# A sixth product in seven quarters, added onto banks that hold a result, with GpSimd adding kept halves

## The chip, the cores and the metric

The kernel runs on one core of a Trainium2 chip. A core has TensorE (PE, matmuls; PEld is its weight loads), VectorE (DVE), ScalarE (ACT), GpSimd (POOL) and SyncE (SP, whose queue issues the DMAs), an on-chip memory (SBUF, 128 partitions) and eight PSUM banks of 128 x 512 fp32, into which matmuls write. The metric is device time in microseconds, the median of several runs; lower is better.

## The reference

```python
def reference(x, w):          # x: 8 x 2048 x 2048, w: 2048 x 2048, float32
    cs = np.cumsum(x, axis=1)
    diff = cs - np.concatenate([zeros, cs[:, :-1, :]], axis=1)
    return np.matmul(diff, w).astype(np.float32)
```

The difference of a running sum is x itself, so what is computed is x times w: 16384 rows by 2048 by 2048.

## The kernel before

The rows are 128 tiles of 128. Four are done plainly, four by `group_plain`, and the remaining 120 by 30 calls of `group(g)`, four tiles each: g, g+1, h = g+2 and h+1. These calls are the periods 1 to 30 of the order list.

**Outer scheme.** The rows are scaled to fp16 and turned (DMA transposes), the right side w is kept in fp16 with one scale. A group multiplies pairs of tiles by the 2 x 2 blocks of w with Strassen's scheme in Winograd's form: seven products with the right sides B11, B21, T1, T2, T3, B22, T4 instead of eight. The left sides are A11, A12, S1, S2, S3, S4, A22, each for g and for h. S1 = A21 + A22, S2 = S1 - A11, S3 = A11 - A21, S4 = A12 - S2, made by DVE (`total`, 128 x 1024 fp16). X and Y are the bank pairs of A11 B11 for g and h; onto these S2 T2 and then S3 T3 are added by matmuls that start with `start=False`. At each stage the value is kept (ACT, `keep`) or added to kept results (DVE, `add`, a scaled add from a bank to SBUF).

**Inner scheme.** Five of the seven products are themselves done in seven quarter products (class `Quarters`, P1 = A11 B11, P2 = A12 B21, P5 = S1 T1, P3 = S4 B22, P4 = A22 T4): the rows g and h make the two rows of blocks, the halves of the depth and of the columns the rest. One product takes seven slots of four matmuls of 128 x 128 by 128 x 512. Its left sums s1 to s4 are made by DVE in small `rooms`; its right-hand differences Q1 to Q4 stand in SBUF (`spare`), or are made anew for each use by `give` into the one buffer `flow`. ACT copies the partial sum in the first bank out (`first`, `out2`, `out4`), DVE adds such copies back into banks (`middle`, `last`).

```python
(h[0], "a11", "t11", True),      # the seven slots of Quarters: bank, left, right, start
(h[1], "s1", "Q1", True),
(h[0], "s2", "Q2", False),
(g[0], "a12", "t21", False),
(h[0], "s3", "Q3", False),
(g[1], "s4", "t22", False),
(h[0], "a22", "Q4", False),
```

The two remaining products, S2 T2 and S3 T3, are whole: the list `steps` of `group` holds their pieces of four matmuls, 16 matmuls for each of S2g T2, S2h T2, S3g T3, S3h T3, and `go` issues the next ones. In period 1 P1 is whole too (`plainly`).

**Rows in.** `load`, `weigh` (ACT, the row's absolute sum, 128 x 1024), `scale_of` (a mean on ACT, a reciprocal on DVE, the unit on ACT), `narrow` (ACT, to fp16) and `turn` (DMA) bring the next group's tiles in. `put` stores results.

**Order.** `record` notes each operation with a label, an engine and a function that issues it; `emit` sorts all of them by a key from the dictionary `places` (by period and label, `None` for the periods without a list of their own), and `after` fixes that order on each engine. So each engine's order is written out by hand, and an engine runs it in order, each instruction behind its own waits.

## Time and profile before

| | |
|---|---|
| runs | 1447.86, 1449.06, 1449.23 us; median 1449.06 us |
| profiled execution | span 1446.9 us from the first to the last instruction; the runs' times lie 1.0 to 2.3 us above it |
| PE, DVE, ACT, POOL busy | 1439.8, 1339.8, 1193.8, 0.9 us |
| granted clock | 0.999 mean |
| DMA | 351.59 MB, mean 243 GB/s |

A row of a table by stretches gives the stretch and its length, the busy time of each engine with its number of instructions, the granted clock, the share of DMA and its rate. A row of a group gives line, engine, operation, what is written and read with shapes, the count, the busy time in us and the mean of one in ns, then the idle time before such instructions and what ended it. A row of the timeline gives start, length and the instruction. Most helpers record through one line, so that L590 is every two-operand DVE operation, L649 the scaled add, L145 and L141 ACT's scaled and plain copies, L602 and L624 the matmuls of whole and of quarter products.

### The profile page before, as it was taken

The numbers are of one execution on the slowest core, as the hardware profiler recorded it, in microseconds if no ns is written. First come the engines' busy times: TensorE is split into PE (matmuls) and PEld (weight loads), VectorE is DVE, ScalarE is ACT, GpSimd is POOL, SyncE is SP. The second block draws the span as 40 slices with busy tenths as digits, with TensorE's granted clock in tenths as the row PEclk, the third lists the DMA queues.
The fourth block names the chain that finished last, engine by engine and source line by source line (L and its number), as shares of the span: only waits on it lengthen the run. The fifth ranks groups of instructions, "written<-read, shape, count | busy, mean of one in ns | idle before, by whom it ended". The sixth has DMA issues, their size and how long they took to land.

```text
span 1446.9 us, 20369 instructions
## 1 busy us (share of the span) xinstructions
PE 1439.8 (100%) x6698; PEld 652.8 (45%) x6698; DVE 1339.8 (93%) x2355; ACT 1193.8 (83%) x1985; POOL 0.9 (0%) x5
## 2 busy tenths in 40 slices
PE   9999999999999999999999999999999999999998
PEld 4444444444444444444444444444444444444443
DVE  7999999999999999999999999999999999999988
ACT  4897878898888888888988888988888888889783
POOL 0000000000000000000000000000000000000000
PEclk9999999999999999999999999999999999999999
DMA  9999988899888999988898989998989998899963
GB/s 362 375 266 265 250 227 222 230 249 264 231 229 223 243 256 241 242 227 229 245 263 219 245 220 242 245 264 217 236 231 242 265 236 237 216 235 249 275 190 116
DMA packets 343930, 351.59 MB, mean 243 GB/s; under 512 B 270992, under 2 KB 270992, under 8 KB 343824
## 3 DMA queue, kind: packets, MB, share of 16 engines
q1 hardware_dynamic: 343824, 350.29, 89.4%
q8 instruction: 52, 0.85, 0.2%
q14 instruction: 54, 0.44, 0.1%
HBM read 150.99 MB, written 134.22 MB: 197 GB/s over the span
## 4 chain that ended last, share of the span: by engine, by line
PE 93%; issue 4%; DVE 1%; ACT 1%; DMA 0%; POOLq 0%; DVEq 0%
PE b L624 61%; PE b L602 32%; DVE W L146 1%; DMA out_dram<-arena 0%; ACT arena L145 0%; DVE arena L649 0%; ACT waste L167 0%; ACT F L145 0%; ACT arena L141 0%; PE b L490 0%; POOLq L1630 0%; DVE b L590 0%; DVEq L1630 0%; ACT b L141 0%; ACT tiny L194 0%
## 5 line engine op out<-in xcount | busy, mean ns | idle before, releaser
L602 PE MATMUL b<-W,x 128*128 128x512 f16 x2144 | 518.3, 379 | 0.0
L649 DVE SCALAR_TENSOR_TENSOR arena<-b,tiny,arena 128x512 f32<-128x512 f32 x612 | 448.0, 747 | 15.0 <-ACT arena L141 4.5
L624 PEld LDWEIGHTS <-arena 128*128 128x128 f16 x2744 | 268.3, 98 | 324.5 <-DVE arena L590 5.4
L624 PE MATMUL b<-W,arena 128*128 128x512 f16 x1672 | 413.8, 379 | 0.0
L145 ACT ACTIVATE arena<-b,tiny 128x512 f32<-128x512 f32 x495 | 316.3, 684 | 31.9 <-PE b L602 13.7
L602 PEld LDWEIGHTS <-x 128*128 128x128 f16 x2144 | 209.7, 98 | 253.1 <-DVE x L590 0.2
L167 ACT ACTIVATE waste<-F,tiny 128x1024 uint8<-128x1024 f32 x246 | 284.0, 1154 | 16.2 <-DMA F<-in_x_dram 14.7
L145 ACT ACTIVATE F<-F,tiny 128x1024 f16<-128x1024 f32 x245 | 280.9, 1147 | 11.7 <-DVE tiny L190 10.6
L624 PE MATMUL b<-W,x 128*128 128x512 f16 x1192 | 288.1, 379 | 0.0
L624 PE MATMUL b<-arena 128*128 128x512 f16 x1072 | 261.6, 379 | 0.1
L624 PEld LDWEIGHTS <-x 128*128 128x128 f16 x1428 | 139.7, 98 | 168.5
L590 DVE TENSOR_TENSOR b<-b,arena 128x512 f32<-128x512 f32 x298 | 206.4, 693 | 5.4 <-ACT arena L141 1.9
L141 ACT COPY arena<-b 128x512 f32<-128x512 f32 (+1 forms) x316 | 181.6, 586 | 27.1 <-PE b L624 16.2
L141 ACT COPY b<-b 128x512 f32<-128x512 f32 x149 | 85.6, 574 | 136.6 <-PE b L624 113.3
L590 DVE TENSOR_TENSOR arena<-W 128x2048 f16<-128x2048 f16 (+1 forms) x158 | 186.0, 1177 | 0.2 <-PE b L624 0.2
L590 DVE TENSOR_TENSOR arena<-x,x 128x512 f16<-128x512 f16 (+1 forms) x181 | 91.9, 508 | 50.5 <-PE b L624 50.4
L590 DVE TENSOR_TENSOR x<-x,x 128x1024 f16<-128x1024 f16 x124 | 85.4, 689 | 1.9
L590 DVE TENSOR_TENSOR arena<-W,arena 128x512 f16<-128x512 f16 (+1 forms) x157 | 86.3, 566 | 0.2 <-PE b L624 0.2
L590 DVE TENSOR_TENSOR arena<-arena 128x512 f16<-128x512 f16 x120 | 50.9, 425 | 13.7 <-PE b L624 11.8
L624 PE MATMUL b<-arena,x 128*128 128x512 f16 x236 | 60.4, 379 | 0.0
L347 PE MATMUL b<-arena 128*128 128x512 bf16 x240 | 53.8, 379 | 0.6 <-DVE arena L142 0.4
L590 DVE TENSOR_TENSOR arena<-x,arena 128x512 f16<-128x512 f16 x119 | 49.9, 419 | 0.3 <-PE b L624 0.3
(51 smaller groups left out, 494.8 us busy)
## 6 DMA issues: line engine op xcount, KB each, us to landing
F<-in_x_dram SPq DMA_DIRECT2D x246, 512.0 KB, 5.5
out_dram<-arena SPq DMA_DIRECT2D x240, 512.0 KB, 4.8
W<-in_w_dram SPq DMA_DIRECT2D x31, 512.0 KB, 9.0
out_dram<-arena SPq DMA_DIRECT2D x31, 256.0 KB, 2.7
W<-in_x_dram SPq DMA_DIRECT2D x16, 256.0 KB, 7.2
x<-F SPq DMA_TRANSPOSE x246, 4.3
arena<-in_x_dram SPq DMA_DIRECT2D x2, 512.0 KB, 5.0
W<-in_w_dram SPq DMA_DIRECT2D x2, 256.0 KB, 9.3
```

The costliest lines, as they stand in the source:

```text
L141: "act": lambda: nc.scalar.copy(to, src),
L145: "act": lambda: nc.scalar.activation(to, src, COPY, scale=scale),
L146: "dve": lambda: nc.vector.tensor_scalar(to, src, scale, None, MUL),
L167: lambda: nc.scalar.activation(waste, data, ABS, bias=least, scale=1.0 / ROW, accum_out=m),
L347: said = nc.tensor.matmul(to[n], xP[:, r, ko, :], b[:, ds(n * NB, NB)], start=(ko == 0), stop=(ko == KO - 1),)
L590: record(label, "dve", lambda: nc.vector.tensor_tensor(dst, p, q, op))
L602: said = nc.tensor.matmul(to[n], a[k], b[k][:, n, :], start=(start and k == 0), stop=(k == KH - 1), skip_group_check=True,)
L624: said = nc.tensor.matmul(to, a[k], b[k], start=(start and k == 0), stop=(k == 3), skip_group_check=True)
L649: label, "dve", lambda: nc.vector.scalar_tensor_tensor(c, p, u, c, MUL, ADD)
```

## The change

S2 T2 becomes P6, in seven slots (class `Onto`). Each slot's quarter is not the start of a result here, since X and Y already hold one: three quarters go straight onto their banks, four go through P2's g banks (`by`), are copied out by ACT (`out0`, `out1`, `out2`, `out4`), and DVE adds the copies into the banks of X and Y (`to`, six adds). Period 1 keeps S2 T2 whole. P6's right sides Q1, Q2 and Q4 take SBUF; Q4 of in3 and in4 has no room of its own any more and is made by `give` for each use. `give` makes Q4 by one instruction instead of four.

C11 + P2 and C22 + X, C22 + Y, eight scaled adds of DVE, become adds of two kept halves on GpSimd (`sum_kept_one`); for C11 + P2 ACT keeps P2's halves first. The sums s1 of P1 and P2 are made by one DVE instruction, and so are their s2 (`first_sums`). In periods 1 to 29 GpSimd makes P4.s1. The four small `unit` products go from ACT to GpSimd. P6 comes before P5, and the S3 T3 pieces stand elsewhere in the order; the `places` lists are new.

```diff
+    all_x = const.tile([P, 4, 2, KH * P], f16, name="x")
     turned_x = [
-        [const.tile([P, KH, P], f16, name=f"x{i}{j}") for j in range(2)] for i in range(4)
+        [all_x[:, i, j].rearrange("p (k m) -> p k m", m=P) for j in range(2)] for i in range(4)
     ]
...
-            record(
-                f"unit{role(t)}",
-                "act",
-                lambda: nc.scalar.activation(u, m, COPY, scale=uw),
-            )
+            record(f"unit{role(t)}", "pool", lambda: nc.gpsimd.tensor_tensor(u, m, uw, MUL))
...
     def tensor(label, dst, p, q, op):
-        record(label, "dve", lambda: nc.vector.tensor_tensor(dst, p, q, op))
+        if label in ('P4.s1',) and 1 <= period[0] <= 29:
+            record(label, "pool", lambda: nc.gpsimd.tensor_tensor(dst, p, q, op))
+        else:
+            record(label, "dve", lambda: nc.vector.tensor_tensor(dst, p, q, op))
...
+    def sum_kept_one(label, c, k):
+        record(label, "pool", lambda: nc.gpsimd.tensor_tensor(c, c, k, ADD))
...
             p, q, op = {"Q1": ("t22", "Q2", SUB), "Q4": ("t21", "Q2", SUB), "Q3": ("Q2", "t11", SUB)}[name]
-            if name == "Q4":
-                less(f"{self.name}.{name}", passed, self.b[p], self.b[q])
-            else:
-                tensor(f"{self.name}.{name}", flow, self.wide[p], self.wide[q], op)
+            tensor(f"{self.name}.{name}", flow, self.wide[p], self.wide[q], op)
...
     def make_3(i):
         t11, t12, t21, t22 = i.t
-        q = i.room()
-        less(f"{i.name}.make1", q, t12, t11)
-        less(f"{i.name}.make2", t12, t22, q)
-        less(f"{i.name}.make4", q, t21, t12)
+        less(f"{i.name}.make1", t12, t12, t11)
+        less(f"{i.name}.make2", t12, t22, t12)
...
+    class Onto:
+        def __init__(self, name, to, by, a, b, right, room, kept):
+            self.name = name
+            self.to, self.by = to, by
+            self.a11, self.a12, self.a21, self.a22 = a.half(0), a.half(1), b.half(0), b.half(1)
+            self.right, self.room, self.kept = right, room, kept
+
+        sum, one, two, three, four = (getattr(Quarters, i) for i in ("sum", "one", "two", "three", "four"))
+
+        def carry(self, i, n, to):
+            p = self.to[to // 2][to % 2]
+            tensor(f"{self.name}.to{to}.{i}", p, p, self.kept[n], ADD)
+
+        def slot(self, i):
+            b = self.right.b
+            (c11, c12), (c21, c22) = self.to
+            to, left, right, start = (
+                (self.by[0], "a11", "t11", True),
+                (self.by[1], "s1", "Q1", True),
+                (self.by[0], "s2", "Q2", False),
+                (c11, "a12", "t21", False),
+                (self.by[0], "s3", "Q3", False),
+                (c12, "s4", "t22", False),
+                (c21, "a22", "Q4", False),
+            )[i]
+            quarter(f"{self.name}.{i}", to, getattr(self, left), b[right], start)
+            if i in (0, 1, 2, 4):
+                n = (0, 1, 2, None, 3)[i]
+                copy(f"{self.name}.out{i}", self.kept[n], to)
+                for c in ((0,), (1, 3), (1,), (), (2, 3))[i]:
+                    self.carry(i, n, c)
...
     def plainly(name, g):
-        return name in {PLAIN + 4: ('P1',)}.get(g, ())
+        return name in {PLAIN + 4: ('P1', 'P6')}.get(g, ())
...
+    def first_sums(g):
+        of = [
+            all_x[:, (t - PLAIN) // 2 % 2 + 2 * (t % 2)].rearrange("p i (n c) -> p n i c", n=2)
+            for t in (g, g + 2)
+        ]
+        P1, P2 = ready[1], ready[2]
+        for n, p, q, op in (
+            (0, of[1][:, 0], of[1][:, 1], ADD),
+            (1, rooms_by[:, 0], of[0][:, 0], SUB),
+        ):
+            tensor(f"P1.P2.s{n + 1}", rooms_by[:, n], p, q, op)
...
-        add("C11g+P2.g", C11g, P2.g, ug, [1])
+        rest = [c[:, n, :] for c in (free[0], free[2]) for n in range(2)] if onto else None
+        if onto:
+            for n in range(2):
+                keep_one(f"keep P2.g.{n}", rest[1 + n], P2.g[n], ug)
+                sum_kept_one(f"C11g+P2.g.{n}", C11g[:, n, :], rest[1 + n])
...
+        if onto:
+            made("P6", in_6, make_5)
+            halves = [chain, rest[1], rest[2], rest[3]]
+            P6 = Onto("P6", (X, Y), P2.g, S2g, S2h, in_6, rooms[0], halves)
+            P6.one()
+            P6.slot(0)
+            P6.slot(1)
+            P6.two()
+            P6.three()
+            P6.slot(2)
+            in_6.give("Q3")
+            P6.slot(3)
+            P6.four()
+            P6.slot(4)
+            P6.slot(5)
+            P6.slot(6)
...
+        in_3.give("Q4")
...
-        add("C22g+X", C22g, X, vg, [1])
+        sum_kept("C22g+X", C22g, C21g, [0])
...
+        in_4.give("Q4")
...
+            first_sums(next_g)
```

The new keys of the periods without a list of their own, where GpSimd's adds and their neighbours stand (a label's key orders it on its engine):

```diff
+            'C11h+P2.h.1': 1601.782, 'P5.s3': 1604.054, 'P6.4': 1604.599, 'in5.Q3': 1604.6,
+            'weigh6.0': 1630.613, 'P5.0': 1642.241, 'C11h+P2.h.0': 1645.842, 'load6.1': 1649.985,
+            'P6.to2.4': 1666.08, 'P6.to1.2': 1667.705, 'S4g': 1670.723, 'P6.3': 1679.028,
+            'P4.s1': 1957.326, 'C12g+X.1': 1958.084, 'keep C22h.1': 1969.538,
+            'keep C12h.1': 1995.823, 'C12h+Y.0': 2011.805, 'S3g T3.0.0': 2028.673, 'P3.2': 2041.921,
+            'P4.2': 2350.472, 'P4.3': 2381.212, 'C22g+X.1': 2438.355, 'P4.out2': 2439.307,
+            'P4.4': 2439.308, 'C12h+P3.h.1': 2442.681, 'P4.middle': 2442.682, 'load7.1': 2449.194,
```

More of the change, by code (lines that the diff above doesn't have):

```diff
@@ L1041, in group @@
         P1.slot(6)
-        if not P5.plain:
-            made("P5", in_5, make_5)
-            in_5.give("Q3")
         C11h = keep("keep C11h", Y, uh, free.pop(1))
         P2.slot(6)
-        add("C11h+P2.h", C11h, P2.h, uh, [0])
         P2.last()
-        add("C11h+P2.h", C11h, P2.h, uh, [1])
-        put(C11h, h, 0)
+        if onto:
+            for n in (1, 0):
+                keep_one(f"keep P2.h.{n}", rest[3 * n], P2.h[n], uh)
+                sum_kept_one(f"C11h+P2.h.{n}", C11h[:, n, :], rest[3 * n])
+        else:
+            add("C11h+P2.h", C11h, P2.h, uh)
+        put(C11h, h, 0)
+        total("S3h", S3h, A11h, A21h, SUB)
+        total("S2h", S2h, S1h, A11h, SUB)
+        if onto:
+            made("P6", in_6, make_5)
[13 more added lines that the diff above has]
+            P6.slot(6)
+            turns = (P2.h, P2.g)
+        else:
+            for one in steps_of(("S2g T2", X, S2g, T2), ("S2h T2", Y, S2h, T2)):
+                matmuls(*one)
+            turns = (P2.h, P2.g)
+        P5 = Quarters("P5", turns, S1g, S1h, in_5, rooms[1])
+        P5.one()
+        P5.two()
+        made("P5", in_5, make_5)
+        in_5.give("Q3")
         P5.slot(0)
@@ L1086, in group @@
         P5.slot(4)
-        if not P3.plain:
-            in_3.give("Q1")
+        in_3.give("Q1")
         P5.last()
@@ L1155, in group @@
         first_two(g + 4)
-        if next_g < END:
-            ready[1].one()
-            ready[1].two()
-        if not P4.plain:
-            in_4.give("Q3")
+        in_4.give("Q3")
         weigh(next_l, [0])
-        go(2)
-        add("C12h+Y", C12h, Y, uh)
-        put(C12h, h, 1)
         turn(next_k, [0])
```

146 lines of the change are left out of this document (58 added, 88 removed), and 783 rows, old and new, of the table places.

## The prediction

> **What bounds the kernel now.** I read the totals first, then a table by stretches, then the chain of waits, and last the groups and single instructions of one period. The first fence is the head of the page and its table of busy times.
>
> ```profile
> span 1446.9 us, 20369 instructions
> ## 1 busy us (share of the span) xinstructions
> PE 1439.8 (100%) x6698; PEld 652.8 (45%) x6698; DVE 1339.8 (93%) x2355; ACT 1193.8 (83%) x1985; POOL 0.9 (0%) x5
> ```
>
> PE is full, DVE nearly, POOL is idle. The span stands 2.2 us below the 1449.06 us median of the runs, so a difference worked out in the trace can be taken off the median as it is. Next the busy times by stretches: two at the start, one period, and 25 periods together (the x counts include an instruction cut at the edge).
>
> ```profile
> core 0: us, PE busy (x) PEld busy (x) DVE busy (x) ACT busy (x) POOL busy (x), PEclk, DMA share, GB/s
> 120.00:164.00 44.00, 44.00 (x206) 19.93 (x204) 43.90 (x96) 35.72 (x61) 0.00 (x0) 1.00 0.91 232
> 164.00:208.00 44.00, 44.00 (x206) 19.89 (x205) 43.05 (x77) 35.13 (x61) 0.00 (x0) 1.00 0.88 243
> 604.02:648.05 44.03, 44.03 (x206) 19.95 (x204) 40.77 (x73) 37.48 (x63) 0.00 (x0) 1.00 0.89 236
> 251.78:1352.79 1101.01, 1100.91 (x5102) 498.83 (x5100) 1019.06 (x1801) 936.55 (x1575) 0.00 (x0) 1.00 0.91 239
> ```
>
> ```profile
> 604.02 12.09 PE b L624 x56
> 648.05 12.09 PE b L624 x56
> ```
>
> The chain returns to the same 56 matmuls every 44.03 us: one call of `group`. In it PE stands still for nothing (1100.91 of 1101.01 us over 25 periods), at the full granted clock of 1.00. The weight loads count the work: 204 per period, so one matmul costs 44.03 / 204 = 0.2158 us. The code gives the same 204: five products of 7 x 4, and four whole ones (S2g T2, S2h T2, S3g T3, S3h T3) of 16. So each matmul removed is worth 0.2158 us as long as DVE and ACT keep up. They have 3.26 and 6.55 us of a period left.
>
> **PE.** S2g T2 and S2h T2 (32 matmuls) become P6 (28). 200 matmuls make 200 x 0.2158 = 43.17 us, 0.86 us less. Period 1 keeps P6 plain, so 29 periods gain: 25.0 us, the most this change can give, and 1424 us if nothing else moves.
>
> **DVE.** The groups of one period:
>
> ```profile
> L649 DVE SCALAR_TENSOR_TENSOR arena<-b,tiny,arena 128x512 f32<-128x512 f32 x21 | 15.4, 747 | 0.5 <-PE b L624 0.2 <-ACT arena L141 0.2
> L590 DVE TENSOR_TENSOR b<-b,arena 128x512 f32<-128x512 f32 x10 | 6.9, 692 | 0.1
> L590 DVE TENSOR_TENSOR arena<-W 128x2048 f16<-128x2048 f16 x5 | 6.1, 1217 | 0.0
> L590 DVE TENSOR_TENSOR arena<-x,x 128x512 f16<-128x512 f16 x4 | 1.7, 417 | 1.9 <-PE b L624 1.9
> L590 DVE TENSOR_TENSOR arena<-W,arena 128x512 f16<-128x512 f16 x4 | 1.6, 418 | 0.0
> L590 DVE TENSOR_TENSOR arena<-x,x 128x1024 f16<-128x1024 f16 x2 | 1.4, 680 | 0.0
> L190 DVE RECIPROCAL tiny<-tiny 128x1 f32<-128x1 f32 x4 | 0.6, 162 | 0.2 <-ACT tiny L188 0.2
> ```
>
> Durations overlap when nothing is waited for, so the price of an instruction on a full engine is the step from its start to the next start. A stretch of the timeline shows it for each kind:
>
> ```profile
> 610.41 0.68 DVE L590 TENSOR_TENSOR arena<-x,x 128x1024 f16<-128x1024 f16 x1
> 611.01 0.42 DVE L590 TENSOR_TENSOR arena<-x,arena 128x512 f16<-128x512 f16 x1
> ...
> 632.03 1.22 DVE L590 TENSOR_TENSOR arena<-W 128x2048 f16<-128x2048 f16 x1
> 633.17 0.42 DVE L590 TENSOR_TENSOR arena<-arena,x 128x512 f16<-128x512 f16 x1
> 633.50 0.42 DVE L590 TENSOR_TENSOR arena<-x,arena 128x512 f16<-128x512 f16 x1
> 633.95 0.70 DVE L590 TENSOR_TENSOR b<-b,arena 128x512 f32<-128x512 f32 x1
> 634.56 0.74 DVE L649 SCALAR_TENSOR_TENSOR arena<-b,tiny,arena 128x512 f32<-128x512 f32 x1
> 635.22 1.22 DVE L590 TENSOR_TENSOR arena<-W 128x2048 f16<-128x2048 f16 x1
> ...
> 640.68 0.16 DVE L190 RECIPROCAL tiny<-tiny 128x1 f32<-128x1 f32 x1
> 640.76 0.40 DVE L590 TENSOR_TENSOR arena<-x 128x512 f16<-128x512 f16 x1
> ```
>
> Steps: 0.60 us for a sum of 1024, 0.33 for one of 512, 1.14 for 2048 (`give`), 0.61 for a bank plus SBUF in place, 0.66 for a scaled add, 0.08 for a reciprocal. Before, by the code: 20 scaled adds, 10 in-bank adds, 6 gives, 8 sums of 1024, 24 of 512, 4 reciprocals: 13.2 + 6.1 + 6.84 + 4.8 + 7.92 + 0.32 = 39.18 us, a floor under the 40.77 seen. The 1.59 us between are small waits for results just made, such as 633.50 to 633.95.
>
> The edits, in steps: eight scaled adds go to POOL, 8 x 0.66 = -5.28. P6 brings six `to` adds into X and Y, 6 x 0.61 = +3.66, four sums, +1.32, and in6.Q3, +1.14. Q4 of in3 and in4 is now made each period, 2 x 1.14 = +2.28. in1.Q4 turns from four pieces to one instruction, 1.14 - 1.32 = -0.18. The first sums of P1 and P2 turn from four to two, 1.20 - 1.32 = -0.12. P4.s1 leaves, -0.33. Together +2.49: the floor rises to 41.67 us, and, if the 1.59 us stay, DVE needs 43.26 us. That is PE's 43.17 us again. So DVE becomes a second bound, and of PE's 0.86 us at least 0.1 is likely lost. Does PE suffer with DVE so full? The two early rows answer: with DVE busy 43.90 and 43.05 of 44.00 us PE was still busy for 44.00. A DVE that is busy throughout has stopped no matmul here, because its sums are ordered well ahead of their slots.
>
> Once, in6 must be made (twelve sums of 512) while in3 and in4 lose four each: +4 x 0.33 = +1.3 us. As these twelve fall mostly on the already full period 2, I take 2 us for all, with 0 and 4 as ends.
>
> **ACT.** Its rows of the same period:
>
> ```profile
> L145 ACT ACTIVATE arena<-b,tiny 128x512 f32<-128x512 f32 x16 | 10.2, 684 | 0.8 <-PE b L602 0.4 <-PE b L624 0.2
> L141 ACT COPY arena<-b 128x512 f32<-128x512 f32 x10 | 5.7, 580 | 0.2
> L141 ACT COPY b<-b 128x512 f32<-128x512 f32 x5 | 2.9, 575 | 4.7 <-PE b L624 4.2 <-DVE tiny L190 0.5
> L194 ACT ACTIVATE tiny<-tiny 128x1 f32<-128x1 f32 x4 | 1.1, 282 | 0.0
> ```
>
> Four more keeps (of P2), 4 x 0.684 = +2.74; four copies of P6's quarters, 4 x 0.580 = +2.32; four units to POOL, -1.13. ACT rises from 37.48 to 41.4 us of 43.17 (96%). Most of its idle time was slack (4.2 us of waits for PE at the copies into a bank), so I charge nothing; its queue now has cover of 1.8 us only. The added waits here: P6's slots 2 and 4 add onto the bank that ACT copies after the slot before, and behind such a copy a `weigh` or `narrow` can be queued. PE has other quarters between; if it hadn't, a period would lose up to one such instruction, about 1.1 us.
>
> **POOL.** Nine two-operand instructions of 512 and four units of 128x1 per period. The nearest rows:
>
> ```profile
> L469 POOL PARTITION_ALL_REDUCE tiny<-tiny x1 | 0.7, 712 | 59.0 <-DVE tiny L465 59.0
> L1619 POOL MEMSET const-bfloat16-1.0<- 128x1 bf16 x1 | 0.1, 101 | 0.0
> ```
>
> One add costs somewhere from 0.7 us (DVE's 692 ns for the same count) to 1.2 us (DVE's 1217 ns for the same count of bytes twice over), so POOL works 6.5 to 11.5 us of 43 and is no bound by itself. Who waits for it: the transfers of C11 and C22, which free buffers, and P4's slot 1 for P4.s1; each has several us. Nothing in the trace of before shows POOL and DVE at work together. Per POOL add the price for DVE lies between 0 (no coupling; a gain is excluded) and its whole 1.2 us. I take 0.1 to 0.2: in the order that the diff gives, several POOL adds (P4.s1, C22g+X.1, both halves of C11h+P2.h) have DVE instructions beside them that read a bank (C12g+X.1 and C12h+Y.0; C12h+P3.h.1 and P4.middle; P6's `to` adds), and these take one SBUF operand. Nine times 0.1 to 0.2 is 0.9 to 1.8, and the 1.59 us of small waits can overlap with it.
>
> The Trainium skill speaks against this move: "SBUF — State Buffer", § Who interferes with whom, says that a Vector instruction with two SBUF inputs contends with a GpSimd one that reads SBUF, and that the second to start is blocked until the first ends. No run here shows it yet; by that rule the sum would be that of the first rival. "GPSIMD Engine Reference", § 3.1, gives 4497 ns for an fp32 add of 2048, so as an estimate about 1.1 us for 512; by it the nine adds take 10 us, inside the bounds above.
>
> **Sum.** A period: DVE's floor 41.67 + about 1.9 for small waits and POOL together = 43.6 us. Gain 44.03 - 43.6 = 0.43 us, x 29 = 12.5 us, less 2 us once: 1449.06 - 10.5 = about 1438.5. Its own bounds: 1424 (PE alone) to 1446.
>
> **First rival, the other side: DVE and POOL take turns.** 10 gives, 10 sums of 1024 and 19 of 512 read two SBUF operands: 11.4 + 6.0 + 6.27 = 23.7 of DVE's 41.67 us. If a POOL add shuts these out for its length, and 57% of DVE's queue is of this kind, an add costs DVE about 0.57 x (0.7 to 1.2) = 0.4 to 0.7 us, nine of them 3.6 to 6.2. Where half of the adds lie beside bank readers it is half that: DVE needs 43.26 + 1.8 = 45.1 at the least and 49.4 at the most. That gives 1480 to 1605 us, likeliest about 1500. It decides early: from (44.03 - 43.26) / 9 = 0.09 us per add the gain is gone, or from (44.03 - 41.67) / 9 = 0.26 us if POOL's blocks hide in the small waits. For it: 57% of DVE's queue, and POOL's adds stand between DVE's. Against it: each add has periods of slack in which to find its place.
>
> **Second rival: three full queues in a row.** All `give`s share the one buffer `flow`, now ten times a period (seven before): matmuls 0.86, give 1.22, hand-over 0.2, ten times 22.8 us; P1's first sums now wait for P4's slots 4 and 5, because one instruction writes the rooms of P1 and P2, and P4 has held one of them. If two to four of these round trips per period miss their slot by 0.3 to 0.5 us each, a period costs 43.6 + 0.9 to 1.5 = 44.5 to 45.1: 1464 to 1480 us. For it: DVE at 100% and ACT at 96% in program order. Against it: the two early rows.
>
> **Third: the losses eat the gain exactly**, a period of 44.0: 1446 to 1452 us.
>
> **How the numbers follow.** Forecast 0.54, taking turns 0.26, full queues 0.13, no change 0.07. A measurement of this kernel can tell about 0.2% (2.9 us) from no change; so faster 0.54, same 0.07, slower 0.39. The forecast's own range is 1424 to 1446. Leaving out the upper part of the first rival (over 1500, 0.15) and little else, the range is 1424 to 1500.
>
> **What would show it.** Right: 200 weight loads in a period of 43.3 to 43.9 us; DVE busy over 98% and PE idle under 0.5 us of it; ACT near 41.4 us; f16 sums still at 417 ns and gives at 1217 ns. Turn-taking would show as f16 sums and gives that grow longer, or start late after the one before, where a POOL add runs, while scaled adds keep 747 ns, and as weight loads that wait for DVE. Full queues would show as waits of PE for ACT's copies or for gives with unchanged durations. The prediction is wrong if the period is above 44.03 us; if it is 43.17 us, I have overcharged DVE.

## The result, and the profile after

The changed kernel takes 1556.13 us (median of 4 runs, 1551.82 to 1563.32) against 1448.69 us of the kernel before on the same chip: ratio 1.0747, 95% interval 1.0719 to 1.0774. It is 107 us slower, where 10.5 us faster was forecast. First the head of its page and its table of busy times.

```profile
span 1555.1 us, 21231 instructions
## 1 busy us (share of the span) xinstructions
PE 1455.3 (94%) x6582; PEld 629.5 (40%) x6582; DVE 1495.2 (96%) x2328; ACT 1297.1 (83%) x2093; POOL 455.1 (29%) x394
```

The matmuls fell from 6698 to 6582, the 29 x 4 that the change removes. But PE went from 100% to 94% of a longer span, and DVE is busy 155 us longer (1495.2 against 1339.8). Where the time went, the table by stretches tells (engine, busy us, number of instructions); the first fence is the kernel after, the second the kernel before.

```profile
core 0: us, PE busy (x) PEld busy (x) DVE busy (x) ACT busy (x) POOL busy (x), PEclk, DMA share, GB/s
0.00:130.00 130.00, 115.02 (x548) 52.70 (x549) 104.74 (x154) 85.11 (x114) 7.83 (x10) 0.95 0.91 295
400.00:1300.00 900.00, 854.19 (x3855) 368.32 (x3854) 884.67 (x1371) 789.82 (x1293) 293.54 (x253) 1.00 0.80 224
```

```profile
0.00:130.00 130.00, 128.01 (x624) 58.75 (x625) 120.64 (x195) 95.02 (x135) 0.90 (x5) 1.00 1.00 323
400.00:1300.00 900.00, 899.90 (x4171) 407.67 (x4169) 831.71 (x1469) 765.22 (x1288) 0.00 (x0) 1.00 0.91 238
```

The matmuls in the 900 us give the period: 900 x 204 / 4171 = 44.0 us before, 900 x 200 / 3855 = 46.7 us after. All periods of runs below are worked out in this way. And 76 matmuls fewer are done in the first 130 us. By the starts of the matmuls in the two traces the 108 us of span (1555.1 less 1446.9) divide into about 16 us ahead of period 1, 5.0 in period 1, 12.5 in period 2, 70 in periods 3 to 29 (27 x 2.6) and 5.1 in the last one, less 0.5 behind the last matmul.

What changed on DVE in these 900 us, by groups (operand shapes, count, busy us, mean ns), in the kernel after:

```profile
L601 DVE TENSOR_TENSOR banks<-banks,arena 128x512 f32<-128x512 f32 x311 | 207.3, 689 | 9.3 <-ACT arena L152 7.2
L601 DVE TENSOR_TENSOR arena<-W 128x2048 f16<-128x2048 f16 x155 | 187.8, 1211 | 0.0
L670 DVE SCALAR_TENSOR_TENSOR arena<-banks,tiny,arena 128x512 f32<-128x512 f32 x231 | 166.4, 740 | 0.0
L601 DVE TENSOR_TENSOR arena<-x 128x512 f16<-128x512 f16 x135 | 85.4, 632 | 0.0
L601 DVE TENSOR_TENSOR x<-x 128x1024 f16<-128x1024 f16 x78 | 61.4, 788 | 0.7
L601 DVE TENSOR_TENSOR arena<-x,arena 128x512 f16<-128x512 f16 x96 | 59.5, 620 | 0.0
L601 DVE TENSOR_TENSOR arena<-arena 128x512 f16<-128x512 f16 x78 | 39.0, 501 | 0.0
L601 DVE TENSOR_TENSOR arena<-arena,x 128x1024 f16<-128x1024 f16 x19 | 20.2, 1063 | 0.0
```

The instructions that read a bank keep their price (692 to 689 ns, 747 to 740). The sums that read two SBUF operands do not: the 512 ones were 417 ns before and are now 451 to 632 in the mean (the group at 451 is not shown), the 1024 ones up to 1063. The gives of 2048 also read two SBUF operands and yet keep their length (1217 to 1211), which needs a reason. A stretch of the timeline (start, length) shows how all this comes about, first POOL, then DVE:

```profile
699.07 3.10 POOL L666 TENSOR_TENSOR arena<-arena 128x512 f32<-128x512 f32 x2 [11.92 <-ACT arena L156]
...
724.22 1.27 POOL L666 TENSOR_TENSOR arena<-arena 128x512 f32<-128x512 f32 x1 [0.29 <-ACT arena L156]
```

```profile
698.56 1.22 DVE L601 TENSOR_TENSOR arena<-W 128x2048 f16<-128x2048 f16 x1
...
701.15 1.30 DVE L601 TENSOR_TENSOR arena<-x,arena 128x512 f16<-128x512 f16 x1
...
723.09 1.30 DVE L601 TENSOR_TENSOR banks<-banks,arena 128x512 f32<-128x512 f32 x2 [0.36 <-ACT arena L152]
724.30 1.46 DVE L601 TENSOR_TENSOR arena<-arena 128x512 f16<-128x512 f16 x1
```

The sum that starts at 701.15, inside POOL's two adds, ends at 702.45, 0.28 us after POOL is done (702.17). The one at 724.30 starts 0.08 us behind a POOL add and ends at 725.76, 0.27 us after it. It is so throughout: of the 70 sums of 512 in the 900 us that start more than 0.15 us before the end of a POOL add or of P4.s1, 69 end 0.28 us after it, and all 33 such sums of 1024 end 0.55 us after it. So the time from POOL's end to theirs does not depend on when they started: they stand until POOL is done. The bank adds at 723.09 beside POOL take 0.65 us each, as ever.

It also goes the other way. The give at 698.56 ends at 699.78, and the first of POOL's two adds, which starts inside it at 699.07, takes 3.10 - 1.27 = 1.83 us instead of 1.27: it ends 1.12 us after the give. All 53 POOL instructions of 512 that start inside a give end 1.12 to 1.14 us after it. No give starts more than 0.02 us before the end of a POOL add here, so the gives are always the first of the two, and it is POOL that stands. This is why their length is as before; the order spares them, not their kind.

This is what the prediction's first rival described, and what it quoted of the Trainium skill ("SBUF — State Buffer", § Who interferes with whom): by that rule the second of the two is blocked until the first ends, and the trace agrees, with 1.46 us for a sum of 0.42 and 1.83 us for a POOL add of 1.27. PE's waits name the receiver (over the 900 us: total, times, longest):

```profile
PEld L635 <- DVE arena L601: 73.1, 95, 2.9
PE banks L635 <- DVE arena L601: 41.8, 60, 2.4
```

### The profile page after: what moved, and what is told of

It is laid out like the page before. It is cut to its first block, busy times and chain, and to the rows that moved or that the text cites. A ratio compares the mean times of both kernels' runs of the same rounds, so it can differ in the third digit from the quotient of the medians.

```text
span 1555.1 us, 21231 instructions
## 1 busy us (share of the span) xinstructions
PE 1455.3 (94%) x6582; PEld 629.5 (40%) x6582; DVE 1495.2 (96%) x2328; ACT 1297.1 (83%) x2093; POOL 455.1 (29%) x394
## 4 chain that ended last, share of the span: by engine, by line
DVE 52%; PE 19%; DMA 12%; issue 11%; ACT 4%; SPq 1%; DVEq 0%; ACTq 0%
DVE arena L601 26%; DVE banks L601 12%; PE banks L635 11%; DVE arena L670 9%; PE banks L613 7%; DVE x L601 5%; DMA x<-F 5%; DMA F<-in_x_dram 4%; PE banks L354 2%; DMA out_dram<-arena 1%; DMA W<-in_w_dram 1%; ACT arena L156 1%; ACT waste L178 1%; ACT arena L152 1%; DMA W<-in_x_dram 1%
## 5 line engine op out<-in xcount | busy, mean ns | idle before, releaser
L666 POOL TENSOR_TENSOR arena<-arena 128x512 f32<-128x512 f32 x236 | 348.1, 1479 | 805.9 <-ACT arena L156 796.8
L635 PE MATMUL banks<-W,arena 128*128 128x512 f16 x2020 | 494.1, 380 | 33.5 <-DVE arena L601 26.0
L156 ACT ACTIVATE arena<-banks,tiny 128x512 f32<-128x512 f32 x611 | 403.5, 696 | 41.5 <-PE banks L613 14.4
L635 PE MATMUL banks<-W,x 128*128 128x512 f16 x1300 | 330.2, 380 | 0.2 <-DVE x L601 0.2
L601 DVE TENSOR_TENSOR banks<-banks,arena 128x512 f32<-128x512 f32 x472 | 314.9, 689 | 12.5 <-ACT arena L152 9.0
L635 PE MATMUL banks<-arena 128*128 128x512 f16 x1188 | 298.3, 381 | 25.5 <-DVE arena L601 21.3
L152 ACT COPY arena<-banks 128x512 f32<-128x512 f32 (+1 forms) x432 | 250.4, 596 | 78.5 <-PE banks L635 45.5
L156 ACT ACTIVATE F<-F,tiny 128x1024 f16<-128x1024 f32 x245 | 282.8, 1155 | 30.3 <-DVE tiny L201 28.8
L613 PE MATMUL banks<-W,x 128*128 128x512 f16 x1216 | 293.8, 379 | 1.6 <-DVE x L601 1.6
L670 DVE SCALAR_TENSOR_TENSOR arena<-banks,tiny,arena 128x512 f32<-128x512 f32 x376 | 271.4, 741 | 0.3
L601 DVE TENSOR_TENSOR arena<-x 128x1024 f16<-128x1024 f16 (+1 forms) x300 | 194.2, 648 | 11.7 <-DMA x<-F 8.9
L635 PE MATMUL banks<-arena,x 128*128 128x512 f16 x476 | 122.9, 381 | 19.4 <-DVE arena L601 19.2
```

The costliest lines, as they stand in the source:

```text
L152: "act": lambda: nc.scalar.copy(to, src),
L156: "act": lambda: nc.scalar.activation(to, src, COPY, scale=scale),
L601: record(label, "dve", lambda: nc.vector.tensor_tensor(dst, p, q, op))
L613: said = nc.tensor.matmul(to[n], a[k], b[k][:, n, :], start=(start and k == 0), stop=(k == KH - 1), skip_group_check=True,)
L635: said = nc.tensor.matmul(to, a[k], b[k], start=(start and k == 0), stop=(k == 3), skip_group_check=True)
L666: record(label, "pool", lambda: nc.gpsimd.tensor_tensor(c, c, k, ADD))
```

## The experiments

"Ratio" is the time over that of the kernel before in the same rounds, with its 95% interval. The waits of single quarter products are worked out from the starts of the matmuls: the gap ahead of a slot beyond the usual 0.216 us, the mean of periods 4 to 28. P6.1 is slot 1 of P6, and so on.

**Are GpSimd's adds the price? Left out, or made to read nothing.** The changed kernel with the adds and P4.s1 dropped, with memsets of the same tiles in their place, and with copies (one operand) in their place.

```diff
-        record(label, "pool", lambda: nc.gpsimd.tensor_tensor(c, c, k, ADD))
+        pass                                                            # no adds
+        record(label, "pool", lambda: nc.gpsimd.memset(c, 0.0))         # writes only
+        record(label, "pool", lambda: nc.gpsimd.tensor_copy(c, k))      # one input
```

> The changed kernel with the eight GpSimd adds and P4.s1 left out altogether; the four units stay. Taking turns for reading: the same as with memsets within 6 us, 1460 to 1480. Turns for any access: clearly below the run with memsets, by 50 us or more. Full queues: above 1515 us as with memsets.

> The changed kernel, with each of GpSimd's nine big instructions per group turned into a memset of the same destination: the eight adds and P4.s1 are left out, GpSimd still writes as much at the same places, and reads nothing. Taking turns for the reading of SBUF: DVE's sums of 512 fall from 0.57 us in the mean to 0.41, DVE's busy time from 45.9 to about 42 us per period, the period from 46.6 to 43.2 to 43.9, and the time to 1460 to 1480 us. Turns for any access: sums and period stay about as they are, 1530 us or more. Full queues (round trips of flow, of ACT's copies and of the first sums): the sums get shorter, but the period stays above 45 us, since the round trips are the same: 1515 us or more.

> The changed kernel with GpSimd copying one operand (the kept half, or P4.s1's first operand) where it added two; the sums are left out so far. Turns for reading: the copies still hold DVE's two-operand sums, but for as long as a copy takes; if that is half of an add, the excess of DVE falls from 3.9 to about 2 us per period and the time to 1515 to 1530. If only GpSimd's two-operand reads collide, the time is that of the run without reads, 1485 to 1495.

| kernel | us | ratio | period |
|---|---|---|---|
| adds left out | 1490.79 | 1.0287 [1.0269, 1.0305] | 44.6 |
| writes only | 1490.90 | 1.0294 [1.0276, 1.0312] | 44.7 |
| one input | 1511.35 | 1.0433 [1.0410, 1.0457] | 45.2 |

The groups of the kernel without adds, same window:

```profile
L601 DVE TENSOR_TENSOR arena<-x 128x512 f16<-128x512 f16 x141 | 59.1, 419 | 9.5 <-PE banks L635 9.5
L601 DVE TENSOR_TENSOR x<-x 128x1024 f16<-128x1024 f16 x80 | 54.7, 684 | 0.7
L601 DVE TENSOR_TENSOR arena<-x,arena 128x512 f16<-128x512 f16 x100 | 41.2, 412 | 0.0
L601 DVE TENSOR_TENSOR arena<-arena 128x512 f16<-128x512 f16 x80 | 33.4, 418 | 0.0
L601 DVE TENSOR_TENSOR arena<-arena,x 128x1024 f16<-128x1024 f16 x20 | 13.5, 674 | 0.0
```

The sums are back at 412 to 419 and 674 to 684 ns. The difference of the means times the counts of after is 28.8 + 8.1 + 20.0 + 6.5 + 7.4 = 70.8 us in 900, over 19.3 periods 3.7 us: 0.41 us of DVE for each of the nine POOL instructions. Memsets on GpSimd cost nothing against leaving them out, and the sums that start inside one keep their length (416 ns for 512); copies, which read one operand, cost 20.6 us; adds, which read two, cost 65.3 us (1556.13 less 1490.79). So it is what GpSimd reads that holds DVE, not that it runs or writes. The copies came out below the 1515 to 1530 us that was expected of turns for reading, and well above the 1495 of no such turns. The first two runs missed as well: the sums fell to 0.41 us as expected of turns, but the period stayed at 44.6 to 44.7 us instead of 43.2 to 43.9, and the time 11 us above 1480. Something else holds the period there, which is the subject of the last experiments.

**The same in the kernel before.** The kernel before with eight GpSimd adds c = c + c per group, each behind one of DVE's scaled adds into C11 and C22; this changes C11 and C22 (doubled).

```diff
+        if label[:6] in ("C11g+P", "C11h+P", "C22g+X", "C22h+Y"):
+            record(f"beside {label}", "pool", lambda: nc.gpsimd.tensor_tensor(c, c, c, ADD))
```

> The kernel before, with eight GpSimd adds per group set on top: each half of C11 and C22 is doubled in place (c = c + c) after DVE's add and ahead of its transfer, so the output has wrong factors there and GpSimd reads two operands of 512 fp32 as after the change. P6 is not in it. Turns: DVE's sums of 512 grow where GpSimd runs, 0.3 to 0.45 us per GpSimd add, so 2.4 to 3.6 us of DVE's 3.3 us of idle time per period; PE stays at 44.0 us or loses up to 1 us: 1449 to 1480 us. If the sums were lengthened by P6's traffic and not by GpSimd, they stay at 418 ns and the time at 1449.

Measured 1515.56 us, ratio 1.0461 [1.0445, 1.0476], 67 us more, although PE, DVE and ACT do exactly the work of before. It was expected at 1480 at the most. Its row by stretches, three groups, two rows of the timeline, and PE's waits for DVE's sums:

```profile
400.00:1300.00 900.00, 869.16 (x3968) 384.54 (x3967) 849.43 (x1404) 734.41 (x1229) 218.57 (x158) 1.00 0.88 228
```

```profile
L649 DVE SCALAR_TENSOR_TENSOR arena<-b,tiny,arena 128x512 f32<-128x512 f32 x386 | 282.4, 743 | 2.5
L590 DVE TENSOR_TENSOR arena<-arena 128x512 f16<-128x512 f16 x80 | 55.3, 692 | 9.3 <-PE b L624 8.0
L590 DVE TENSOR_TENSOR arena<-W 128x2048 f16<-128x2048 f16 x96 | 126.1, 1313 | 0.0
```

```profile
735.41 1.04 POOL L652 TENSOR_TENSOR arena<-arena 128x512 f32<-128x512 f32 x1 [1.29 <-DVE arena L649]
735.85 1.68 DVE L590 TENSOR_TENSOR arena<-W 128x2048 f16<-128x2048 f16 x1
```

```profile
PEld L624 <- DVE arena L590: 36.0, 59, 1.1
PE b L624 <- DVE arena L590: 12.4, 20, 0.6
```

Here some gives start behind a POOL add, and they are held like the sums: the one at 735.85 ends at 737.53, 1.08 us after POOL (736.45), and so do all 20 that start inside an add. The period is 900 x 204 / 3968 = 46.3 us. This shows more than the price. DVE is busy 849 of 900 us, the time that it stands included, so it has 50 us of idle time left, and PE still loses 2.2 us per period, with 48 us of waits for DVE's sums in the 900. What PE loses is not DVE's load over its capacity but the lateness of single sums.

**The adds back on DVE.** DVE takes the halves from the bank again by its scaled add, ACT keeps nothing of P2, and P4.s1 is DVE's: once with each add at the place of ACT's keep, once (periods 3 to 28) with its key between the bank's last write and its next use. In the first, in a few of the periods with a list of their own, an add stands ahead of the keep that fills its operand, so what is added there is not the reference's; the count of adds is whole. What the second computes is not the reference's either, and the reason was not found.

```diff
-                keep_one(f"keep P2.g.{n}", rest[1 + n], P2.g[n], ug)
-                sum_kept_one(f"C11g+P2.g.{n}", C11g[:, n, :], rest[1 + n])
+                add_one(f"C11g+P2.g.{n}", C11g[:, n, :], P2.g[n], ug)
```

> P6 without GpSimd's adds: C11 + P2 and C22 + X, Y are scaled adds of DVE from the bank again, ACT keeps nothing of P2, and P4.s1 is DVE's. By start-to-start steps DVE needs 41.67 + 8 x 0.66 + 0.33 = 47.3 us per period, 1.6 us more with small waits. Taking turns: no sum is lengthened, DVE bounds, period 47.3 to 48.9 us, time 1575 to 1625. That is slower than the changed kernel, so that the adds on GpSimd were worth having even at their price. If GpSimd's adds cost DVE more than they save (5.6 us per period), the time falls below 1556.

> P6 with C11 + P2 and C22 + X, Y as scaled adds of DVE from the bank in periods 3 to 28 (ACT keeps nothing of P2 there, P4.s1 is DVE's), with their keys held between the last write of the bank and its next use; periods 1, 2, 29 and 30 as in the changed kernel. In the first try at this, all those adds stood right behind ACT's keeps and the period was 52.2 us with DVE busy 48.1 of it. DVE needs 47.3 us by steps. Taking turns: nothing lengthens the sums, DVE bounds at 48 to 50 us, 1590 to 1650 us, above the changed kernel, so the adds on GpSimd still saved more than they cost. If it falls below 1556, they did not.

Measured 1706.81 us, ratio 1.1787 [1.1769, 1.1804], and 1696.77 us, ratio 1.1703 [1.1673, 1.1732]; periods of 52 us. Both missed badly, far above the 47 to 50 us of period that DVE's load gave. In the second, the largest wait of PE's matmuls over the 900 us is for the scaled adds themselves:

```profile
PE banks L635 <- DVE arena L673: 96.2, 51, 3.6
```

Part of the longer period is the clock: the granted clock is 0.96 in these 900 us and 0.98 in those of the first, against 1.00 in the changed kernel. In these two orders, where each bank is written again soon, the adds on DVE cost more than GpSimd's turns do. Whether they would in an order made for them is not shown.

**The start.** The changed kernel begins with another order of its first casts, weighings and products, and 16 us later. First the order list of before for this part; then also the first rows' weighing behind the last cast of w; then that without GpSimd's adds.

```diff
+            if at == 0 and label in early:          # the list of before
+                return early[label] - 20
...
+    places[0].update({'weigh0.0': 142.7, 'weigh0.1': 142.71, 'mean0': 142.72, 'scale0': 142.73, ...})
```

> The changed kernel with one edit: the operations up to the end of the first plain products (loads, casts, turns, maxima, plain.0) stand in the order of the kernel before; everything else keeps the new order. In the traces period 1 starts 15.8 us later after the change. If the new order list alone did that, period 1 starts about 16 us earlier and the time falls from 1556 to about 1540 us. If it came with something else (GpSimd's instructions, chance in the loads), the time stays within 5 us of 1556. Neither the theory of turns between DVE and GpSimd nor that of full queues expects a change of the period, 46.6 us in the mean of periods 3 to 29.

> The changed kernel with the old order up to the first plain products, as in the first run, and with weigh0 and weigh2 (and what follows from them: mean0, scale0, mean2, narrow0.0) keyed behind the last cast of w. In the trace of the first run ACT stood 10.35 us before its first weigh, for a load of x, with casts of w queued behind it, and PE 8.5 us for those casts. If the early weigh is the second half of the lost start, period 1 starts at 119 to 122 us after the first matmul as in the kernel before (131 to 137 in the changed one), and the time falls to 1538 to 1546 us. If the start is limited by the loads themselves, it stays at 1551 to 1558.

> The same start, and the eight GpSimd adds and P4.s1 left out. If the start and the turns are separate costs, they add: 1490.8 - 15 = 1474 to 1478 us, still above the kernel before, because the period without turns is 44.7 and not 43.2 us. If the late start had hidden something else, the gain is under 8 us.

Measured 1556.51 us, ratio 1.0741 [1.0725, 1.0757]; 1557.27, 1.0750 [1.0725, 1.0775]; 1481.93, 1.0229 [1.0214, 1.0245]. In the kernel after PE stands at the 30th microsecond for a cast of x (first row); with the old list that is gone, but ACT then stands for rows coming in, and PE waits behind it (second fence, PE and ACT):

```profile
30.62 1.03 PE L300 MATMUL banks<-waste,W 128*128 128x128 bf16 x8 [6.62 <-DVE W L153]
```

```profile
61.48 19.51 PE L401 MATMUL banks<-arena 128*128 128x512 bf16 x79 [8.49 <-ACT arena L152]
59.26 1.15 ACT L178 ACTIVATE waste<-F,tiny 128x1024 uint8<-128x1024 f32 x1 [10.35 <-DMA F<-in_x_dram]
```

The list of before alone brings about 4 us of the start. With the weighing late as well, period 1 starts 6.4 us earlier than in the kernel after (128.9 against 135.3 us behind the first matmul; 119.1 before). With GpSimd's adds that gain does not reach the end: periods 3 to 29 take it back (5.8 us more in the sum). Both times lie where no gain was expected, and hide that the start did move. Without the adds the gain does reach the end: 8.9 us less than the same kernel with the start as changed (1490.79).

The traces say where the 16 us of the kernel after go. PE stands twice, 6.62 us at 30.62 (above) and 5.17 us at 65.79, and in a stretch of 6.8 us that begins in each stop the granted clock is 0.50; before it is 1.00 in these 130 us:

```profile
65.79 9.37 PE L354 MATMUL banks<-arena 128*128 128x512 bf16 x34 [5.17 <-ACT arena L152]
```

```profile
28.70:35.50 6.80, 4.88 (x23) 2.68 (x23) 6.17 (x9) 0.00 (x0) 0.00 (x0) 0.50 1.03 410
62.80:69.60 6.80, 3.81 (x10) 1.34 (x10) 6.80 (x8) 6.04 (x8) 0.00 (x0) 0.50 1.02 401
```

Half of the 4.88 + 3.81 us in which PE is busy at half the clock is 4.3 us, as an estimate; with the two stops that makes 16.1 us. With the list of before and the weighing late one such stop is left, for a cast on DVE, with half the clock from 66.0 to 72.9 us. It makes up most of the 10 us of later start that are still there:

```profile
69.51 9.14 PE L401 MATMUL banks<-arena 128*128 128x512 bf16 x34 [5.92 <-DVE arena L153]
```

**Why 44.7 and not 44.0 or less, without the adds.** First DVE's load: on the kernel without adds, the two added gives of Q4 left out (old contents used), and four of P6's six bank adds left out.

```diff
-        in_3.give("Q4")
+        in_3.b["Q4"] = passed           # and in_4
...
-                for c in ((0,), (1, 3), (1,), (), (2, 3))[i]:
+                for c in ((0,), (), (1,), (), ())[i]:
```

> The changed kernel without the eight GpSimd adds and P4.s1 (as in the run that left them out: 1490.8 us, period 44.69 us, DVE busy 42.35), and also without the two new gives, in3.Q4 and in4.Q4: slot 6 of P3 and of P4 multiplies what stands in flow. DVE has 2.28 us per period less, and two of the ten refills of flow are gone. Full queues by round trips of flow: the period falls by 0.8 us or more, towards 43.2 to 43.9, 1445 to 1468 us. DVE's load as such: also down, by the same amount as in the run without four of the to adds. Neither: within 8 us of 1490.8.

> The same base without GpSimd's adds, and four of P6's six to adds left out (those of the quarters of slots 1 and 4): DVE has 4 x 0.61 = 2.44 us per period less, as much as without the two gives, but the refills of flow stay ten and the copies stay. DVE's load as such: the period falls as without the two gives, to 43.2 to 43.9, 1445 to 1468 us. Round trips of flow: it stays within 8 us of 1490.8.

Measured 1482.37 us, ratio 1.0229 [1.0212, 1.0246], period 44.4; and 1490.45, 1.0294 [1.0279, 1.0310], period 44.7. Four adds fewer, 2.1 us of the 42.4 us that DVE is busy per period, change nothing at all. DVE's load is not what holds the period. Without the two gives, which take about as much off DVE, the time falls by 8.4 us, less than the full queues were expected to give; most of it is the wait ahead of P2.4, 0.26 us shorter per period.

Then the order. Without the adds PE waits 0.81 us per period ahead of P6.1 and 0.54 ahead of P2.4. Three sums moved so that P6's come earlier, without and with GpSimd's adds (the latter on the repaired start):

```diff
+    places[None].update({'P5.s1': 1496.277, 'P5.s2': 1496.278, 'P2.s3': 1250.0})
```

> The changed kernel without GpSimd's adds (1490.8 us, period 44.69 us), with three keys of DVE's list changed and nothing left out besides: P5.s1 and P5.s2 stand behind P6.s1 and P6.s2, and P2.s3 ahead of S2g and in1.Q4. In the trace of the base PE waits in two places of a period, 0.81 us ahead of P6's slot 1 and 0.54 us ahead of P2's slot 4; P6.s1 is DVE's sixth sum in a row there, two of them for P5, and P2.s3 stands behind a give. If the order of these sums is what keeps the period above 43.2 us, the first wait falls by 0.5 to 0.7 us and the second by 0.2 to 0.5, the period to 43.6 to 44.0, the time to 1461 to 1476 us. If the waits come from ACT's copies or from the turned rows, they stay: 1485 to 1495.

> The changed kernel whole, with GpSimd's adds, with the repaired start (old order of the first products, weigh behind the casts) and the same three keys changed. The waits ahead of P6's slot 1 and P2's slot 4 were 1.01 and 0.14 us here, and 2.4 us per period stand elsewhere (P4's slot 6, P6's slot 4, P3's slot 1). If order and turns add up, 0.5 to 0.8 us per period go: 1532 to 1546 us; if a DVE that is held up by GpSimd is late at the next place whatever the order, it stays at 1550 to 1560.

Measured 1505.77 us, ratio 1.0401 [1.0384, 1.0418], and 1624.69, ratio 1.1217 [1.1201, 1.1234]: slower by 15 and by 67 us than the same kernels without the moves, and above every branch of what was expected. P2.s3 now stands at the head of DVE's queue and waits for its room:

```profile
L601 DVE TENSOR_TENSOR arena<-x 128x512 f16<-128x512 f16 x140 | 58.5, 418 | 32.9 <-PE banks L635 32.3
```

32.3 us of such idle time in the window, 1.6 us per period (9.5 in all without the move), stand in front of every sum behind it; with the adds there is more behind it. The two P5 sums alone:

```diff
+    places[None].update({'P5.s1': 1496.277, 'P5.s2': 1496.278})
```

> The changed kernel without GpSimd's adds (left out: the sums that GpSimd made of kept halves and the fourth product's first left sum), and of the three moves of the earlier run only two: the fifth product's sums P5.s1 and P5.s2 stand right behind P6.s2 on VectorE's list; P2.s3 keeps its place. If the wait of the first quarter product of P6 (0.81 us per period without the adds) comes from the place of these two sums ahead of P6's, it falls to about 0.2 us, the period from 44.7 to about 44.1 us and the time to 1470 to 1482 us. If not (P5 then waits for its own sums, or P6's wait has another giver), the period stays at 44.5 to 45.0 us and the time at 1485 to 1497 us.

Measured 1499.43 us, ratio 1.0354 [1.0337, 1.0371], period 45.0: P6.1's wait stayed at 0.76 us. Its rows say why (DVE's sum P6.s1, ACT's copy of P2's half, PE's P6.1):

```profile
1011.63 0.42 DVE L601 TENSOR_TENSOR arena<-x 128x512 f16<-128x512 f16 x1
```

```profile
1011.66 0.71 ACT L156 ACTIVATE arena<-banks,tiny 128x512 f32<-128x512 f32 x1
1012.42 1.89 PE L635 MATMUL banks<-W,arena 128*128 128x512 f16 x8 [0.60 <-ACT arena L156]
```

P6.s1 ends at 1012.05, 0.37 us before P6.1 starts. ACT's copy ends at 1012.37, 0.05 us before, and so it does in nearly every period. In the kernel without the moves both end 0.06 and 0.10 us before P6.1: the page names DVE, which came last by 0.04 us, but taking DVE away only brings out ACT. That copy is one that the change adds, and ACT makes it behind a narrowing of 1.18 us. The next three runs move ACT's instructions: the narrowing behind the copy and P2.out2 ahead of a weighing, with and without the P5 sums, and with GpSimd's adds.

```diff
+    places[None].update({'narrow4.1': 1480.49, 'P2.out2': 1246.0})
```

> As the run before (GpSimd's adds and its first left sum left out, P5.s1 and P5.s2 behind P6.s2), and on ScalarE two moves: the second narrowing goes behind the copy of P2's half (keep P2.g.1) that P6's first quarter product waits for, and P2's copy P2.out2 goes ahead of the second weighing. In the run before P6.1 starts 0.05 us after that copy ends in every period, and P2.4 0.05 us after P2.out2. If ScalarE's order is what is left, P6.1's wait (0.76 us) and P2.4's (0.62 us) go, the period falls from 45.0 to 43.6 to 43.9 us and the time to 1460 to 1472 us. If the loss only turns up at another wait, the period stays above 44.5 us and the time above 1485 us.

> GpSimd's adds and its first left sum left out; only ScalarE's two moves, VectorE's order as in the change. P2.4's wait (0.54 us) goes, P6.1's stays at about 0.75 us, because without the moves of P5's sums VectorE's sum ends only 0.04 us before ScalarE's copy did. Period from 44.7 to 44.1 to 44.3 us, 1472 to 1480 us. If ScalarE's order is not the cause: no change, 1487 to 1495 us. If VectorE's sums don't matter at all: the same as the run with both moves.

> The whole change with GpSimd's adds, with the repaired start, P5's two sums behind P6's and ScalarE's two moves. If the 4 us per period of taking turns is a price of its own, the period stays at 45.3 to 46.2 us (46.6 less what the two waits cost) and the time at 1520 to 1545 us, still slower than before; if the turns only hurt through these two waits, it falls to 44 us and 1470 us.

Measured 1522.63 us, ratio 1.0506 [1.0489, 1.0524]; 1518.02, 1.0486 [1.0468, 1.0504]; 1603.03, 1.1064 [1.1048, 1.1081]. All three are slower than without the moves. The first lies in its branch of a loss that turns up elsewhere, the other two outside all that was expected. A row of the second:

```profile
1116.25 0.59 ACT L152 COPY arena<-banks 128x512 f32<-128x512 f32 x1 [3.60 <-DMA out_dram<-arena]
```

P2.out2 goes into a tile whose result is still being stored; where it was, the instructions ahead of it covered this. Now ACT stands for 3.6 us there, and a new wait of 1.3 us appears ahead of P1.6. The last run touches no shared tile: S3h behind P6's sums on DVE, the narrowing behind the copy on ACT.

```diff
+    places[None].update({'S3h': 1496.277, 'narrow4.1': 1480.49})
```

> GpSimd's adds and its first left sum left out, and two moves that leave every shared buffer as it is: on VectorE S3h goes behind P6's sums (0.7 us earlier for P6.s1), on ScalarE the second narrowing goes behind the copy of P2's half (1.2 us earlier for that copy). Both givers of P6.1's wait (0.81 us) are then ahead of it. If that wait is a loss by itself, it falls under 0.2 us, the period from 44.7 to 44.0 to 44.2 us and the time to 1470 to 1478 us. If the loop through ScalarE and VectorE is what holds PE, so that the time turns up at the next wait, P6.1's wait falls but the period stays above 44.5 us and the time above 1484 us.

Measured 1494.21 us, ratio 1.0302 [1.0284, 1.0319], period 45.0. P6.1's wait fell from 0.81 to 0.33 us, but P6.2 waits 0.40 and P5.2 0.24 us, where they had 0.01 and 0.09, and P2.4 0.66. Its rows of PE and of ACT:

```profile
1098.68 1.04 PE L635 MATMUL banks<-W,arena 128*128 128x512 f16 x4
1099.99 1.02 PE L635 MATMUL banks<-W,arena 128*128 128x512 f16 x4 [0.28 <-ACT arena L152]
```

```profile
1098.33 1.14 ACT L156 ACTIVATE F<-F,tiny 128x1024 f16<-128x1024 f32 x1
1099.37 0.57 ACT L152 COPY arena<-banks 128x512 f32<-128x512 f32 x1
```

The narrowing now stands ahead of the next copy (P6.out0), which ends at 1099.94, and P6.2 starts at 1099.99. The wait moved by one slot. This is the second branch of that expectation. Shown: the wait ahead of P6.1 is not a loss of its own; half of it went, and the period did not fall. For P2.4 this is not shown, since the moves that shortened its wait also brought the wait for a tile that is being stored. Open: which round trip between PE, ACT and DVE sets the 44.7 us; no order was found that does better.

## Why the prediction was wrong, point by point

**PE's saving was right and small.** 200 matmuls per period, 116 fewer in all, 0.86 us each period. Everything else had to stay under that.

**The step that failed: the price of a GpSimd add, taken at 0.1 to 0.2 us of DVE.** It measured 0.41 us, inside the first rival's 0.4 to 0.7 and far over that rival's thresholds (0.09 and 0.26). The reason given for the low value was that bank readers stand beside the adds. That these lose nothing was right (740 and 689 ns). But the adds run where ACT's keep lets them, not where the list has them, and DVE's two-operand sums stand there too. Part of the price is the order: half of the two-operand work that the first rival counted is gives (11.4 of 23.7 us), and none of them was held, because each came first. The adds were also longer than the bound of 1.2 us, which came from DVE's rows: 1.27 us where they wait for nothing, and in the mean, with the time that they themselves stand behind DVE,

```profile
L666 POOL TENSOR_TENSOR arena<-arena 128x512 f32<-128x512 f32 x236 | 348.1, 1479 | 805.9 <-ACT arena L156 796.8
```

The estimate of 1.1 us from the Trainium skill ("GPSIMD Engine Reference", § 3.1) lies between the lengths of an add that waits for nothing, 1.27 us here and 1.04 us for c = c + c in the kernel before; it leaves out the standing. The measurements decide.

**The argument "DVE at 43.90 of 44.00 us and PE did not stop" failed.** It was read as proof that a full DVE is harmless. The kernel before with GpSimd's adds has DVE idle for 50 of 900 us and loses 2.2 us per period. A busy share says nothing of when a sum is due. For the same reason the sum of the prediction had the wrong path: it let DVE's load set the period (41.67 us and small waits). Without the adds the period was 44.7 us with DVE busy 42.4 of it, and a lighter DVE did not move it.

**The first rival's mechanism held, and its time was too low.** The period that it gave, 45.1 to 49.4 us, holds the measured 46.7; but its "likeliest 1500" took the lower end, and nothing was added for the start and for the order. The adds alone cost 65 us, of which by the starts of the matmuls 52 lie in periods 3 to 29, 8 in period 2 and 4 in the last one.

**The second rival came true beside it, not in its place.** Without the adds the period is 44.6 to 44.7 us, inside its 44.5 to 45.1, with its signs: PE waits for ACT's copies and for sums, and no duration has grown. The place is not the one it named, though: leaving out the two gives of Q4 brought back 8.4 us of 42, and a lighter DVE brought nothing. The prediction gave each rival a chance as if only one could happen; they added up. The range ended at 1500 because of this and because the upper part of the first rival was left out of it.

**ACT charged at nothing: not borne out, but its price is open.** Its busy time came out as forecast (819.59 us in 900 without the adds, over 20.2 periods 40.7 us; forecast 41.4). But the prediction's own "if not" (up to 1.1 us behind a weighing or a narrowing) is what stands at P6.1: a keep that the change adds, behind a narrowing of 1.18 us. What this costs by itself no run shows, since moving the narrowing away only moved the wait.

**The start was not priced at all.** Period 1 starts 16 us later, by two stops of PE and the halved clock that goes with them, and periods 1 and 2, where P6's right sides are made, are 3.7 and 4.9 us longer without the adds, where 2 us once were charged. These are about 25 of the 42 us that are left without GpSimd's adds; 27 x 0.65 = 17.5 are the longer periods.

## What to carry to other kernels

Before an elementwise step goes to GpSimd, count which of VectorE's instructions read two SBUF operands and how long the GpSimd instruction is: each such pair that meets with GpSimd first costs VectorE what is left of the GpSimd instruction, with VectorE first it is GpSimd that stands, and VectorE's idle time does not pay for it, because one late sum stops TensorE at once. An edit that saves 2% of the matmuls in a kernel whose order was fitted by hand has to be priced with its new order, the start included; when a wait has two givers within 0.1 us, the profile names only the later one. Rivals with different mechanisms are added up before the range is closed.

## What the runs showed of the hardware

- A VectorE sum of two SBUF operands that starts during a GpSimd add stands until the add is done: 1.46 us for 0.42, ending 0.27 us behind it. A GpSimd add that starts during such a VectorE instruction stands in turn: 1.83 us for 1.27. Instructions with one operand in a bank are untouched (0.65 us beside an add), and GpSimd memsets hold nothing.
- By the groups of the runs, in the mean, a GpSimd instruction of 128 x 512 fp32 took 1479 ns as an add in the changed kernel and 1376 ns in the kernel before, 784 ns as a copy and 524 ns as a memset; one of 128 x 1 took 616 ns. All but the memset hold time that GpSimd stood behind VectorE: where it waited for nothing, the add took 1.27 us (1.04 in the kernel before) and the copy 0.61.
